# The gate of the first half step: sixteen float32 gate products on TensorE, replaced by row products that VectorE sums

## The chip, the cores and the metric

The kernel runs on one core of a Trainium2 chip. The metric is the device time of one execution in microseconds (us); a lower one is better. Times of several runs are given as their median with the lowest and the highest. One execution was taken by the hardware profiler; all rows below come from it.

## The reference

A two-layer backbone works on 512 latent tokens and 256 context tokens of width 1024, all in float32. Each layer is a half step of a gated feed-forward net, an attention (2-D neighbourhood attention in layer 0, windowed attention in layer 1), and a second half step. Each of these three is modulated by a shift, a scale and a gate, which come from one conditioning vector per stream (latent `c`, context `c_ctx`):

```
m = split(silu(c) @ w_mod[i] + b_mod[i], 9)            # nine vectors of 1024 per layer and stream
y = (silu(a) * v) @ w_out,  [a, v] = (h*(1 + m[1]) + m[0]) @ w_in
h = layer_norm(alpha*h + 0.5 * m[2] * y)               # m[2]: the gate of the first half step
```

The case is about `m[2]` of layer 0. It is a vector of 1024 for each of the two streams. It isn't needed to compute `y`, but it is needed to add `y` to `h`.

## The kernel before

All activations lie transposed in SBUF: 8 tiles of 128 features, 768 token columns each. The weights are streamed as units of 128 x 2048, each in four quarters of 256 KB; a quarter is loaded (L94), cast to a high part by ScalarE (L102) and a low part is taken off by GpSimd (L104). A product in float32 accuracy is three matmuls, high x high, high x low and low x high (L153 to L155). The high and low parts lie in rings of eight quarters each, so a new unit can be prepared only when an old one has been read to its end.

A half step (`ffn`) goes through the inner width in 11 chunks. A chunk has two units that give the `a` and `v` products (`av`, tiles `pa` and `pv`), of which the gated value `gh`/`gl` is made, and a third unit for the way down (`down`, tiles `pd`). Each of the eight output tiles of `down`, for each group of columns, is added to the stream `z` by VectorE with the gate as a factor (`accumulate`, L453). So the first instruction that needs the gate `m[2]` is the first accumulate of chunk 0. PSUM has eight banks, by tag: "mm" and "c" two each for `pa` and `pv`, "s" two, "t" and "o" one each. In this half step the outputs of `down` in chunk 0 go through "s", "s" and "t".

The modulation vectors are made in two ways. The first (`gemv`) multiplies on TensorE: a stationary 128 x 32 piece with both conditioning vectors, a moving 128 x 512 weight tile, eight products in four column strips; then ScalarE copies the bank out (L176), four small matmuls transpose it (L179), and VectorE adds the bias (L182). The shift and scale of the first half step are made like this before anything else can run. Its gate also is: `late_gate` calls `gemv_bg(0, 4)` and `gemv_bg(0, 5)`, for 512 columns each. These load eight tiles of 256 KB each into the six "t2" buffers (L189) and multiply at L172 into the bank "o".

The second way (`gemv_dve`) leaves TensorE alone. The weights lie transposed in memory, so a tile holds 128 outputs by 512 inputs. A conditioning row is loaded to all partitions into one of two "ln" buffers (L223), Silu puts it into a PSUM bank (L225; latent into "o", context into "t"), and VectorE multiplies tile and row and sums along the row in one instruction (L208):

```
x = nc.vector.tensor_tensor_reduce(out=junk[:], in0=w[:], in1=cb[st], scale=1.0, scalar=0.0,
                                   op0=ALU.mult, op1=ALU.add, accum_out=out[st])
```

`junk` is scratch, in the same two "ln" buffers. Each output tile takes one such product per stream and per half of the 1024 inputs. All products of one half run before the rows of the other half are loaded. The products are a queue `bg` that `tick()` works off, at a pace that spreads them over the chunks; outside the middle chunks (phase "T") their tiles use the "t2" buffers, inside it two buffers "wt" and `zspare`. Before, the remaining 48 vectors' tiles (24 to 71) of layer 0 are queued ahead of the first half step, 192 products in two batches, and the first are worked off in chunk 1.

The order of the work on each engine is written down before the run: the framework simulates the program, lets instructions that stand earlier in it go first among those that are ready in the simulation, and fixes each engine's order. SP issues nearly all loads, in such an order. After chunk 1, `bias_tables` loads a table for the attention through SP: 8 small loads (`xd`), then 16 broadcast copies in memory (`yd`, 252 KB each).

Of the kernel before, what the change touches and what calls it, by code (L numbers as in the profile page):

```python
# [38 lines left out]
def hybrid_kernel(ctx: ExitStack, tc: tile.TileContext, h0, cc, crow, wmod, wmodt, bmod, lnp, wst,  # L39
                  rpbp, nmask, sinks, ropec, rmat, ident, wmask, out):  # L40
    nc = tc.nc
# [8 lines left out]
    def bank(tag, nm):  # L50
        return pp.tile([P, 512], F32, tag=tag, name=nm, bufs=banks[tag])

    def t2(nm, tag="t2"):
        return tp.tile([P, 512], F32, tag=tag, name=nm, bufs={"t2": 6, "ln": 2, "sl": 2}[tag])
# [109 lines left out]
    def gemv(layer, ch, pieces, tag):  # L164

        nm = f"{layer}_{ch}"
        ps = bank(tag, f"gm{nm}")
        kt = 0
        for t in pieces:
            for j in range(t.shape[1]):  # L170
                q = kt % 4
                nc.tensor.matmul(ps[32 * q:32 * q + 32, :], c_sb[:, kt, :], t[:, j, :], start=kt < 4, stop=kt >= 4,  # L172
                                 tile_position=(0, 32 * q))
                kt += 1
        ev = t2(f"gev{nm}")
        nc.scalar.copy(ev[:], ps[:])  # L176
        pt = bank(tag, f"gt{nm}")
        for j in range(4):
            nc.tensor.matmul(pt[:, 2 * j:2 * j + 2], ev[:, j * P:(j + 1) * P], sel[:], start=True, stop=True)  # L179
        for a in range(2):  # L180
            t = ch * 2 + 8 * a if ch < 4 else ch * 4 + 2 * a
            nc.vector.tensor_tensor(out=mod[layer][:, t:t + 2, :], in0=pt[:, 4 * a:4 * a + 4].rearrange("p (t s) -> p t s", s=2),  # L182
                                    in1=bmod_sb[:, layer, t:t + 2, None].broadcast_to([P, 2, 2]), op=ALU.add)

    def gemv_bg(layer, ch):
        pieces = []
        for q in range(8):
            t = t2(f"wm{layer}_{ch}_{q}").rearrange("p (a b) -> p a b", a=1)
            nc.sync.dma_start(t[:], wmod[ch, q // 4, :, q % 4:q % 4 + 1, :])  # L189
            pieces.append(t)  # L190
        gemv(layer, ch, pieces, "o")

    bg, last, last_exp, wtq = [], [None], [None], [0]

    def gemv_dve(layer, *ranges):


        def products(t, half, cb, out):
            wtq[0] += 1
            nm = f"wt{layer}_{t}_{half}"  # L200
            if phase_of[0] != "T":
                w = t2(nm)
            else:
                w = zspare if wtq[0] % 3 == 0 else ph["T"].tile([P, 512], F32, tag="wt", name=nm, bufs=2)
            nc.sync.dma_start(w[:], wmodt[layer, t, half])
            for st in sorted(out):
                junk = t2(f"jk{layer}_{t}_{half}_{st}", "ln")
                x = nc.vector.tensor_tensor_reduce(out=junk[:], in0=w[:], in1=cb[st], scale=1.0, scalar=0.0,  # L208
                                                   op0=ALU.mult, op1=ALU.add, accum_out=out[st])
                behind(x, last[0])  # L210
                yield

        def steps():
            cb, now = {}, None
            for i, (t0, t1, streams) in enumerate(ranges):
                acc = tp.tile([P, 48, 2, 2], F32, tag="gacc", name=f"ga{layer}_{t0}", bufs=1)[:, 0:t1 - t0]
                for half in ((0, 1), (1, 0))[i % 2]:
                    if half != now:
                        now, cb = half, {}
                        for st in streams:  # L220
                            nm = f"cb{layer}_{t0}_{half}_{st}"
                            t = t2(nm, "ln")
                            nc.sync.dma_start(t[:], crow[st, half:half + 1, :].broadcast_to([P, 512]))  # L223
                            cb[st] = bank("ot"[st], nm)[:]
                            behind(nc.scalar.activation(cb[st], t[:], AF.Silu), last_exp[0])  # L225
                    for t in range(t0, t1):
                        yield from products(t, half, cb, {st: acc[:, t - t0, half, st:st + 1] for st in streams})
                n = len(streams)
                nc.vector.tensor_tensor(out=acc[:, :, 0, 0:n], in0=acc[:, :, 0, 0:n], in1=acc[:, :, 1, 0:n], op=ALU.add)
                nc.vector.tensor_tensor(out=mod[layer][:, t0:t1, 0:n], in0=acc[:, :, 0, 0:n],  # L230
                                        in1=bmod_sb[:, layer, t0:t1, None].broadcast_to([P, t1 - t0, n]), op=ALU.add)

        bg.append((sum(2 * len(st) * (t1 - t0) for t0, t1, st in ranges), steps()))

    pace = [0.0, 0.0]

    def tick():

        pace[1] += pace[0]
        while bg and pace[1] >= 1:  # L240
            pace[1] -= 1
            if next(bg[0][1], "end") == "end":
                bg.pop(0)
# [25 lines left out]
    def gate(layer, m, w):  # L269
        gt = cp.tile([P, DT, 2], F32, name=f"gt{layer}_{m}")  # L270
        nc.vector.tensor_scalar(out=gt[:], in0=mvec(layer, m), scalar1=w, scalar2=None, op0=ALU.mult)
        return gt
# [49 lines left out]
    def behind(x, y):  # L322

        if y is not None and x.ins.engine == y.ins.engine:
            tc.add_manual_dep(x.ins, y.ins.name, mybir.DependencyInfo(
                mybir.DependencyClass.NoSync, mybir.DependencyReason.DATA), reason="order")
# [489 lines left out]
    def constants():  # L816
        for t, src in ((lnp_sb, lnp), (nmask_sb, nmask), (rm_sb, rmat)):
            behind(nc.sync.dma_start(t[:], src[:]), loaded[0])
        nc.sync.dma_start(nsink[:], sinks[:].broadcast_to([P, NH]))
        nc.vector.tensor_scalar(out=nsink[:], in0=nsink[:], scalar1=-1.0, scalar2=None, op0=ALU.mult)  # L820
# [333 lines left out]
    with tc.tile_pool(name="pre", bufs=1) as fp:  # L1154
        open_av()
        for q in range(4):
            pieces = []
            for i in range(2):
                t = fp.tile([P, 4, 512], F32, tag="wm", name=f"wm0_{q}_{i}", bufs=7)
# [75 lines left out]
            write(norm)  # L1235

    def late_gate():
        for ch in (4, 5):
            gemv_bg(0, ch)
        constants()  # L1240

    def whole(x, head):

        return lambda gi: [f() for f in (x[:5] if gi == 0 else head)]
# [4 lines left out]
    l3 = [ln("l3", i, g, 1, 0, 1, 3, "o", True) for i, g in enumerate(g2)]  # L1249
    l4 = [ln("l4", i, g, 1, 1, 1, 6, ("mm", "o")[i]) for i, g in enumerate(g1)]  # L1250

    gemv_dve(0, (24, 40, (0, 1)), (40, 72, (0, 1)))
    ffn("0a", g2, lambda: gate(0, 2, 0.5), late_gate, whole(l0[0], l0[1][:1]), first,
        {(f, g): ps for f in range(2) for g, ps in zip(g2, opened[f])})
    plan(pq0_0_0=l0[1][1:2], pk0_1_0=l0[1][2:3], vn0_1=l0[1][3:5] + l0[0][5:] + l0[1][5:])
# [140 lines left out]
```

## Time and profile before

| | us |
|---|---|
| median of 3 runs | 2860.63 |
| lowest, highest | 2854.68, 2862.81 |
| the profiled execution, its own time | 2868.23 |
| its span | 2866.4 |

| engine | busy us | share of the span |
|---|---|---|
| TensorE, matmuls | 2728.1 | 95% |
| TensorE, weight loads | 2447.8 | 85% |
| VectorE | 1805.4 | 63% |
| ScalarE | 1213.4 | 42% |
| GpSimd | 1658.0 | 58% |

The span is the time from the first to the last instruction of the profiled execution; the execution's own time has a little around it. PE is TensorE with its matmuls, PEld its weight loads, which overlap them; DVE is VectorE, ACT ScalarE, POOL GpSimd, and SPq the queue in which SP issues transfers. PEclk is the granted clock of TensorE as a share of 2.4 GHz. In a row of the timeline, what stands in brackets is how long the engine was idle before, and what ended that. A float32 matmul of the gate is two instructions in the trace. Starts of matmuls are closer together than their durations, since they are pipelined.

### The profile page before, as it was taken

The page shows a single profiled execution, that of the slowest core. Times are in us where ns is not written, and L with a number is a line of the kernel's source. Part 1 is how long each engine was busy: PE and PEld are TensorE (multiplying, and loading weights), DVE is VectorE, ACT ScalarE, POOL GpSimd, SP SyncE. Part 2 cuts the span into 40 slices and gives each one's busy share as a digit, 9 for nine tenths or more (in the row PEclk, how much of TensorE's full clock was granted, in tenths as well). Part 3 has the DMA queues.
Part 4 walks back from the last instruction along what each step waited for, and adds up shares of the span by engine and source line. Part 5 has one row for each costly group of instructions (what it writes and reads, how often), then busy time and mean ns, then how long its engine had stood idle before and what let it go on. Part 6 is the DMA issues. An engine that isn't in the chain of part 4 may idle for free.

```text
span 2866.4 us, 48106 instructions
## 1 busy us (share of the span) xinstructions
PE 2728.1 (95%) x17122; PEld 2447.8 (85%) x17122; DVE 1805.4 (63%) x4124; ACT 1213.4 (42%) x2497; POOL 1658.0 (58%) x1488
## 2 busy tenths in 40 slices
PE   8999999999999989999999999999998998899997
PEld 5789899888888878999998899998886776888997
DVE  3286777585545676766654776666566667687744
ACT  4223333256454444434333534343246555444443
POOL 4357575375434455876744677765466444577763
PEclk9999999999999989999999999999999999899998
DMA  8525557432212212345462326466522111235562
GB/s 300 141 87 158 133 144 208 134 103 82 60 49 62 58 56 86 97 121 140 119 167 83 96 83 166 134 183 180 174 81 62 31 31 45 59 89 129 123 181 65
DMA packets 286016, 322.42 MB, mean 112 GB/s; under 512 B 28497, under 2 KB 174033, under 8 KB 284753
## 3 DMA queue, kind: packets, MB, share of 16 engines
q1 hardware_dynamic: 269936, 290.89, 34.2%
q0 software_dynamic: 15552, 28.32, 5.9%
q8 instruction: 135, 2.21, 0.3%
q14 instruction: 105, 0.85, 0.1%
q10 hardware_dynamic: 288, 0.14, 0.0%
HBM read 311.41 MB, written 12.25 MB: 113 GB/s over the span
## 4 chain that ended last, share of the span: by engine, by line
PE 52%; DVE 6%; DMA 2%; issue 2%; ACT 1%; POOL 1%; SPq 0%; DVEq 0%; POOLq 0%; ACTq 0%
PE pd1a L153 2%; PE pd0b L153 2%; PE pd1a L154 2%; PE pd0b L154 2%; PE pd0b L155 2%; PE pd1a L155 2%; PE wo L800 1%; PE pd1b L153 1%; PE pd1b L154 1%; PE pd1b L155 1%; DMA wr<-in_wst_dram 1%; PE tpw L791 1%; PE pa1a L153 1%; PE pa1a L154 1%; PE pv1a L153 1%
## 5 line engine op out<-in xcount | busy, mean ns | idle before, releaser
L104 POOL TENSOR_TENSOR wl<-wr,wh 128x512 fp32r<-128x512 f32 x308 | 404.0, 1328 | 298.4 <-ACT wh L102 238.4
L104 POOL TENSOR_TENSOR wl_s<-S,wh_s 128x512 fp32r<-128x512 f32 x202 | 268.4, 1366 | 60.5 <-ACT wh_s L102 59.7
L102 ACT CAST wh<-wr 128x512 fp32r<-128x512 f32 x308 | 186.7, 619 | 215.1 <-DMA wr<-in_wst_dram 62.2
L102 ACT CAST wh_s<-S 128x512 fp32r<-128x512 f32 x216 | 130.9, 620 | 322.4 <-POOL S L574 84.1
L208 DVE CUSTOM_DVE_ANT_0 jk<-wt,cb 128x512 f32<-128x512 f32 x303 | 200.4, 680 | 61.4 <-DMA wt<-in_wmodt_dram 52.1
L574 POOL TENSOR_TENSOR S<-wr,wr 128x512 f32<-128x512 f32 x108 | 146.9, 1360 | 148.6 <-DMA wr<-in_wst_dram 130.1
L104 POOL TENSOR_TENSOR wl_a<-wr,wh_a 128x512 fp32r<-128x512 f32 x120 | 159.1, 1376 | 24.9 <-ACT wh_a L102 24.5
L102 ACT CAST wh_a<-wr 128x512 fp32r<-128x512 f32 x162 | 100.4, 621 | 125.9 <-PE pd1b L154 18.3
L453 DVE SCALAR_TENSOR_TENSOR z<-pd0b,gt,z 128x256 f32<-128x256 f32 (+1 forms) x176 | 103.4, 602 | 62.2 <-PE pd0b L155 62.0
L453 DVE SCALAR_TENSOR_TENSOR z<-pd1a,gt,z 128x512 f32<-128x512 f32 (+1 forms) x168 | 99.8, 619 | 44.5 <-PE pd1a L155 43.3
L807 POOL TENSOR_SCALAR p<-p,l 128x512 f32<-128x512 f32 x64 | 44.6, 698 | 128.9 <-DVE l L906 120.5
L453 DVE SCALAR_TENSOR_TENSOR z<-pd0a,gt,z 128x512 f32<-128x512 f32 (+1 forms) x168 | 98.7, 618 | 29.5 <-PE pd0a L155 28.9
L319 POOL TENSOR_SCALAR z<-z,ag_None,ab_None 128x256 f32<-128x256 f32 (+1 forms) x78 | 63.5, 819 | 53.4 <-DVE uh L305 42.8
L208 DVE CUSTOM_DVE_ANT_0 jk<-zspare,cb 128x512 f32<-128x512 f32 x113 | 75.8, 679 | 15.6 <-DMA zspare<-in_wmodt_dram 15.6
L807 POOL TENSOR_SCALAR pw<-pw,l 128x512 f32<-128x512 f32 (+1 forms) x64 | 41.2, 645 | 74.4 <-DVE l L1097 33.0
L574 POOL TENSOR_TENSOR S<-S,wr 128x512 f32<-128x512 f32 x54 | 77.1, 1427 | 3.2 <-DVE x1b L557 0.7
L574 POOL TENSOR_TENSOR S<-wr,S 128x512 f32<-128x512 f32 x54 | 76.8, 1422 | 2.9
L905 ACT ACTIVATE p<-s,m 128x512 f32<-128x512 f32 x64 | 44.0, 688 | 77.3 <-DVE m L903 72.3
L453 DVE SCALAR_TENSOR_TENSOR z<-pd1b,gt,z 128x512 f32<-128x512 f32 (+1 forms) x98 | 56.8, 609 | 14.8 <-PE pd1b L155 12.3
L306 DVE TENSOR_TENSOR ul<-ufl,uh 128x256 fp32r<-128x256 f32 (+1 forms) x88 | 63.0, 722 | 2.3 <-ACT ufl L301 1.7
L301 ACT ACTIVATE ufl<-z,bi_None,sc_None 128x256 f32<-128x256 f32 (+1 forms) x86 | 54.7, 654 | 22.2 <-DVE z L438 21.9
L153 PE MATMUL pd0a<-gh0a,wh 128*128 128x512 f32 (+1 forms) x144 | 50.6, 365 | 8.3 <-DVE z L453 8.3
(1463 smaller groups left out, 10687.0 us busy)
## 6 DMA issues: line engine op xcount, KB each, us to landing
wr<-in_wst_dram SPq DMA_DIRECT2D x524, 256.0 KB
wt<-in_wmodt_dram SPq DMA_DIRECT2D x175, 256.0 KB
zspare<-in_wmodt_dram SPq DMA_DIRECT2D x65, 256.0 KB
wr_0b<-in_wst_dram SPq DMA_DIRECT2D x42, 256.0 KB
wr_1b<-in_wst_dram SPq DMA_DIRECT2D x42, 256.0 KB
wr_2b<-in_wst_dram SPq DMA_DIRECT2D x42, 256.0 KB
wr_3b<-in_wst_dram SPq DMA_DIRECT2D x42, 256.0 KB
wm<-in_wmod_dram SPq DMA_DIRECT2D x8, 1024.0 KB
```

The lines of the kernel that those rows point to most:

```text
L102: nc.scalar.copy(hi[:], src[:])
L104: eng.tensor_tensor(out=lo[:], in0=src[:], in1=hi[:].bitcast(F32), op=ALU.subtract)
L153: nc.tensor.matmul(ps, a[0], b[0], start=first, stop=False)
L154: nc.tensor.matmul(ps, a[0], b[1], start=False, stop=False)
L155: last_pe[0] = nc.tensor.matmul(ps, a[1], b[0], start=False, stop=last)
L208: x = nc.vector.tensor_tensor_reduce(out=junk[:], in0=w[:], in1=cb[st], scale=1.0, scalar=0.0, op0=ALU.mult, op1=ALU.add, accum_out=out[st])
L301: nc.scalar.activation(uf[:, :n], zs, AF.Identity, scale=s1, bias=s2)
L306: return hi, nc.vector.tensor_tensor(out=lo, in0=uv, in1=uo.bitcast(F32), op=ALU.subtract)
L319: nc.gpsimd.tensor_scalar(out=zs, in0=zs, scalar1=prm[2][:, d:d + 1], scalar2=prm[3][:, d:d + 1], op0=ALU.mult, op1=ALU.add)
L453: last[0] = nc.vector.scalar_tensor_tensor(out=zt(d, c0, c1), in0=pd, scalar=gt[:, d, st:st + 1], in1=zt(d, c0, c1), op0=ALU.mult, op1=ALU ...
L574: nc.gpsimd.tensor_tensor(out=t[:], in0=a[:], in1=b[:], op=o)
L807: nc.gpsimd.tensor_scalar(out=p, in0=p, scalar1=r, scalar2=0.0, op0=ALU.mult, op1=ALU.add)
```

## The change

The gate is no longer made by `gemv_bg`, which goes. `late_gate` puts the eight output tiles 16 to 23 (the gate's 1024 outputs) with both streams into the queue of VectorE's products, sets the pace to one product per tick and works the queue off on the spot: 32 products, with two rows loaded for each half. Only then come the constants and the queueing of the other 192 products, which stood ahead of the half step before. In the program all of this stands ahead of chunk 0.

```
-    def gemv_bg(layer, ch):
-        pieces = []
-        for q in range(8):
-            t = t2(f"wm{layer}_{ch}_{q}").rearrange("p (a b) -> p a b", a=1)
-            nc.sync.dma_start(t[:], wmod[ch, q // 4, :, q % 4:q % 4 + 1, :])
-            pieces.append(t)
-        gemv(layer, ch, pieces, "o")
...
     def late_gate():
-        for ch in (4, 5):
-            gemv_bg(0, ch)
+        gemv_dve(0, (16, 24, (0, 1)))
+        pace[0] = 1
+        while bg:
+            tick()
         constants()
+        gemv_dve(0, (24, 40, (0, 1)), (40, 72, (0, 1)))
...
-    gemv_dve(0, (24, 40, (0, 1)), (40, 72, (0, 1)))
     ffn("0a", g2, lambda: gate(0, 2, 0.5), late_gate, whole(l0[0], l0[1][:1]), first,
```

## Rows read from the trace of the kernel before

**Rows 1.** The page, its first part: busy time of each engine, share of the span.
```profile
PE 2728.1 (95%) x17122; PEld 2447.8 (85%) x17122; DVE 1805.4 (63%) x4124; ACT 1213.4 (42%) x2497; POOL 1658.0 (58%) x1488
```

**Rows 2.** Stretches of 20 us: length, busy us (instructions), PEclk, DMA share, GB/s.
```profile
core 0: us, PE busy (x) PEld busy (x) DVE busy (x) ACT busy (x) POOL busy (x), PEclk, DMA share, GB/s
60.00:80.00 20.00, 20.00 (x92) 12.21 (x90) 3.60 (x7) 6.25 (x13) 7.73 (x6) 1.00 0.42 120
80.00:100.00 20.00, 20.00 (x102) 13.76 (x101) 1.62 (x4) 2.16 (x4) 3.87 (x4) 1.00 0.32 97
100.00:120.00 20.00, 20.00 (x107) 16.60 (x106) 8.15 (x16) 6.08 (x11) 12.93 (x13) 1.00 0.50 80
...
140.00:160.00 20.00, 17.61 (x74) 14.35 (x75) 17.79 (x46) 3.37 (x6) 5.16 (x5) 0.73 0.62 200
```

**Rows 3.** Groups of TensorE's instructions from 60 to 110 us: busy us, mean ns.
```profile
L172 PE MATMUL gm<-wm,c_sb 128*32 128x512 f32 x32 | 12.4, 603 | 0.0
...
L179 PE MATMUL gt<-sel,gev 128*128 128x2 f32 x16 | 1.9, 240 | 0.0
```

**Rows 4.** TensorE in order of time, 63 to 110 us: start us, duration us, instruction.
```profile
63.28 0.28 PE L155 MATMUL pa0a<-uh,wl 128*128 128x256 f32 x1
63.41 0.28 PE L153 MATMUL pa0a<-uh,wh 128*128 128x256 f32 x1
63.61 1.05 PE L172 MATMUL gm<-wm,c_sb 128*32 128x512 f32 x2
64.59 0.38 PE L154 MATMUL pa0a<-ul,wh 128*128 128x256 f32 x1
...
74.70 0.39 PE L153 MATMUL pd0a<-gh0a,wh 128*128 128x512 f32 x1
74.93 0.40 PE L154 MATMUL pd0a<-gl0a,wh 128*128 128x512 f32 x1
...
92.39 0.39 PE L153 MATMUL pv0a<-uh,wh 128*128 128x512 f32 x1
92.70 1.91 PE L172 MATMUL gm<-wm,c_sb 128*32 128x512 f32 x12
94.55 0.50 PE L154 MATMUL pv0a<-ul,wh 128*128 128x512 f32 x1
...
103.20 0.40 PE L153 MATMUL pa0a<-uh,wh 128*128 128x512 f32 x1
...
109.07 0.40 PE L153 MATMUL pd0a<-gh0a,wh 128*128 128x512 f32 x1
```

**Rows 5.** TensorE in order of time, the first matmul after the stop.
```profile
141.89 0.80 PE L153 MATMUL pd0a<-gh0a,wh 128*128 128x512 f32 x1 [6.83 <-DVE z L453]
```

**Rows 6.** VectorE in order of time: the gate, two products, the product that waits.
```profile
105.61 0.24 DVE L271 TENSOR_SCALAR gt<-mod 128x16 f32<-128x16 f32 x1
...
125.97 0.69 DVE L208 CUSTOM_DVE_ANT_0 jk<-wt,cb 128x512 f32<-128x512 f32 x1 [0.67 <-ACT cb L225]
...
126.58 0.68 DVE L208 CUSTOM_DVE_ANT_0 jk<-wt,cb 128x512 f32<-128x512 f32 x1
...
140.13 0.69 DVE L208 CUSTOM_DVE_ANT_0 jk<-wt,cb 128x512 f32<-128x512 f32 x1 [9.65 <-DMA wt<-in_wmodt_dram]
```

**Rows 7.** SP's queue in order of time: start us, time to the end of the issues.
```profile
43.10 0.62 SPq L223 DMA_DIRECT2D cb<-in_crow_dram  x1
...
48.12 1.40 SPq L189 DMA_DIRECT2D wm<-in_wmod_dram  x2
...
71.18 5.99 SPq L94 DMA_DIRECT2D wr<-in_wst_dram  x4
...
116.46 12.21 SPq L826 DMA_DIRECT2D yd<-xd  x14
129.53 0.87 SPq L205 DMA_DIRECT2D wt<-in_wmodt_dram  x1
```

**Rows 8.** A stretch of 4 us, columns as in the 20 us stretches.
```profile
60.00:64.00 4.00, 4.00 (x24) 3.25 (x23) 2.42 (x5) 3.04 (x7) 2.59 (x2) 1.00 0.25 69
```

## The prediction

> **What bounds the kernel now.** I read the busy shares first: TensorE is busy for 95% of the span, VectorE for 63%, ScalarE for 42% [rows 1]. A share over the whole span does not say what a change in one stage is worth, so the second view is the table of 20 us stretches, for the stretch that the change touches. The reader is to see that TensorE is busy for all of the 60 us from 60 to 120 at a granted clock of 1.00, while VectorE works 3.60, 1.62 and 8.15 us of each 20 [rows 2]. Here TensorE is the bound and VectorE has 35 us to spare in the 40 us from 60 to 100 (40 - 3.60 - 1.62). The third view is TensorE's instructions in order of time. In this stretch one matmul starts as the one before lets it, 0.13 us apart at 256 columns (63.28 to 63.41) and 0.23 us at 512 (74.70 to 74.93), and nothing else comes between them but the gate's own products [rows 4]. So each of these that goes lets all that follows move forward.
>
> The first place where TensorE stops is at 134.7 us: the next matmul starts at 141.89, after 6.83 us of idle time that ends with an accumulate of VectorE (L453) [rows 5]. That accumulate stood in VectorE's queue behind a row product (L208) which began at 140.13, after 9.65 us of waiting for its weight tile [rows 6]. The clock fell to a mean of 0.73 in the stretch from 140 to 160 [rows 2].
>
> **The change part by part.** *Removed from TensorE:* 16 gate products, each in two passes, so 32 instructions of L172 in the stretch from 60 to 110, and two groups of eight small transposing matmuls at L179; they are busy for 12.4 and 1.9 us there [rows 3]. The busy time is the lower bound of what they take, 14.3 us; the gap that they make between their neighbours is the better measure. A single product: the matmul at 63.41 is followed by one at 64.59 instead of 0.13 us later, and that one lasts 0.38 us instead of 0.28, so 1.18 - 0.13 + 0.10 = 1.15 us [rows 4]. Ten of the 16 stand alone like this, by the twos in which L172 comes: 11.5 us. Six run together at 92.70 (x12): 92.39 to 94.55 is 2.16 us, less 0.23, and 0.11 for the longer neighbour: 2.0 us [rows 4]. The two transposing groups are taken at their busy time, 1.9 us [rows 3]. The sum is 11.5 + 2.0 + 1.9 = 15.4 us, all of it in time in which TensorE never waits.
>
> *Added to VectorE:* 16 weight tiles, each multiplied with two conditioning rows, 32 products. Two that follow each other start 0.61 us apart (125.97, 126.58) [rows 6], so 32 x 0.61 = 19.5 us. The cover is VectorE's 35 us of idle time [rows 2]; I cost them at nothing. With that cover gone, as where accumulates are due, each product delays one by 0.61 us.
>
> *Transfers:* 16 tiles of 256 KB go and 16 of the same size come, into the same six buffers. New are four broadcasts of the conditioning rows (two streams, two halves), each with a Silu into the banks "o" and "t". The rings are 25% busy from 60 to 64 us [rows 8], so I cost this at nothing; the wait that it could make is weighed next.
>
> *When the gate comes.* Before, it is there at 105.61 [rows 6]. After, the loads can be issued where the gate's loads stood, from 48.12 [rows 7]; the rings fall quiet at about 61 [rows 8], so the first half's 16 products run from about 61 to 71 (16 x 0.61). The second half's rows need the "ln" buffers that the products also use as scratch, so their loads are issued only then, on SP and behind the weight loads that hold it from 71.18 for 5.99 us: about 77 [rows 7]. No row shows how long such a load takes to land; it is bounded below by nearly nothing and above by 10.6 us, the time from the tile load issued at 129.53 to the product at 140.13 [rows 6, 7]. With 9.8 us for the second half the gate comes at 87 to 98; I take the early half, as the traffic of 60 to 64 is nearer to that at 77 than that of 130.
>
> *What TensorE does meanwhile.* Before, it ran from 63.41 to 109.07 without needing the gate; without 15.4 us of gate products it reaches the same point at 93.7 [rows 4]. Left then, before it must have the gate, is the rest of the second unit of the next chunk: 48 matmuls at 0.23 and 48 at 0.13 us, 17.3 us, of which some 5 lay between 103.20 and 109.07 [rows 4]. So its supply lasts to about 93.7 + 12 = 106, less 1.4 us for the one output tile (6 x 0.23) that can no longer use bank "t" so early: 104. The gate comes 6 to 17 us before that. The bound of this cost is nothing on one side and, on the other, what the slower rival below prices.
>
> *Moved:* the queueing of the 96 further products in two batches now stands behind the first 32. Their rows were loaded at 43.10 [rows 7], long before use; now they wait for the same scratch buffers, until the gate's products end, at 87 to 98. The second row needs bank "t", which the down products also use and which came free at about 125 (first product with it at 125.97 [rows 6]), so 110 in the new order; 12 us and more lie between, against a landing of at most 10.6. I cost it at nothing. SP's constants move behind the products and are used much later: nothing.
>
> *The stall at 134.7.* Its transfers (16 broadcast copies of the bias table, 14 of which hold SP from 116.46 for 12.21 us, with the next tile load at 129.53 behind them [rows 7]) follow weight loads that follow TensorE's progress, so I let the stall move with all the rest. Its price is 6.83 us of idle time [rows 5] and the clock: a mean of 0.73 over 20 us means 10.8 us at the lower level of 1.2 GHz (0.27 / 0.5 x 20), of which TensorE was idle for 2.4, so 8.4 us of work at half speed cost 4.2 us more [rows 2]. That is 11.0 us that the new order can give back, and I take none of it.
>
> *Sum.* The profiled execution took 2868.2 us with a span of 2866.4; less 15.4 gives 2852.8. The median of the three runs is 2860.6, 7.6 lower; less the same 15.4 it gives 2845.2. I predict 2845.
>
> **The rivals.**
>
> *Faster still.* Accumulates and products meet differently and the stall at 134.7 goes too. For it: the gate comes earlier than TensorE's own forward shift explains (up to 18 us against 15.4), so the first chunk's outputs leave bank "t" sooner and the next products can start ahead of the bias table's traffic. Against it: three tiles are all that can be loaded ahead, and the rest meets that traffic anyway. 2845 - 11 = 2834.
>
> *Most of it given back.* TensorE comes sooner to data that does not come sooner. For it: the tile load of 129.53 is paced by SP and by other transfers; if the product at 140.13 and the accumulate behind it do not move, or the second half of the gate lands late, TensorE idles for what it saved. Against it: the loads follow the release of weight buffers by TensorE itself. With half of 15.4 and the clock's 4.2 lost: 2845 + 8 + 4 = 2857, within 0.3% of before. The Trainium skill has a rule on this side (Perfetto Trace Analysis, "Identifying the Most-Contended Engine"): a high busy share of matmuls is a poor measure of closeness to the bound, and the share of weight loads is better. By that rule TensorE, whose weight loads are busy 12.21 of 20 us from 60 to 80 [rows 2], would have slack there and the removal would return nothing, 2860.6; the unbroken starts in [rows 4] speak against it, and it adds little to this rival's chance.
>
> *Slower.* The order on each engine is fixed before the run. If TensorE's order puts down products that need the gate ahead of the next chunk's products, it stands still until the real gate comes, however much other work there is. Place: the first accumulate after the gate. Price: the gate needs two loads in a row, the second half's rows and its last tiles; if both are as late as the wait of 9.65 us [rows 6], the idle time is 19.3 us, and the clock costs 4.2 more as at 140: 2845.2 + 23.5 = 2868.7, slower than before. It decides from 15.4 - 4.2 = 11.2 us of idle time on. For it: just this happened at 134.7, with one load. Against it: the rings are much quieter at 77. The Trainium skill says that VectorE's queue is strictly first in, first out (PSUM — Partial Sum Buffer, "Engine vs sequencer instructions"); the accumulate behind the product of 140.13 agrees, and the rule speaks for this rival.
>
> **How the numbers follow.** My forecast has a chance of 0.47, faster still 0.17, given back 0.22, slower 0.14. The forecast's own range is 2839 to 2851 (the stall a few us longer or shorter). The whole range reaches from 2831 (the full 11 us and 3 of spread) to 2866, which leaves out the worse part of the slower case. This kernel's measurement can tell 0.3%, 8.6 us, from no change: below 2852 is faster, 0.47 + 0.17 = 0.64; 2852 to 2869 the same, 0.22; slower 0.14.
>
> **What would show it.** Right: no L172 or L179 on TensorE after 50 us; TensorE busy without a gap from 60 to about 119; 32 products of L208 before the first accumulate, most between 60 and 98; the gate (L271) at 87 to 98; and the first matmul of each later stage 13 to 18 us earlier. Wrong: idle time of TensorE ahead of the first down products whose wait ends on VectorE; a product that waits for a row's Silu for more than 10 us; a stall near 119 longer than 6.83 us; or a shift of the later stages below 9 us.

## The result and the profile after

The changed kernel took 2844.02 us (median of 5 runs, 2841.37 to 2846.08) beside 2862.71 us for the kernel before: a ratio of 0.9939, 95% interval 0.9922 to 0.9956. A second series gave 2847.86 us (2846.78 to 2849.40) beside 2859.08, ratio 0.9962 [0.9949, 0.9975]. By these ratios the gain is 17 us in the first series and 11 us in the second; 2845 us was predicted, 15.4 us of gain.

The profiled execution took 2845.25 us with a span of 2843.3 us. In the changed kernel the lines past the removed function are 8 lower: the products are L200, the conditioning rows are loaded at L215 and put through Silu at L217, the gate is L263, the accumulate L445. The busy shares of the page, as in [rows 1]:

```profile
PE 2705.9 (95%) x17074; PEld 2440.1 (86%) x17074; DVE 1835.1 (65%) x4186; ACT 1215.3 (43%) x2499; POOL 1656.7 (58%) x1488
```

The shares hardly move: a gain of 0.5% in one stage can't be read from them. The table of 20 us stretches shows it, with the columns of [rows 2]:

```profile
60.00:80.00 20.00, 20.00 (x115) 17.55 (x114) 13.96 (x43) 6.20 (x12) 6.37 (x5) 1.00 0.69 221
80.00:100.00 20.00, 20.00 (x116) 17.57 (x116) 15.26 (x38) 7.05 (x14) 18.09 (x17) 1.00 0.54 100
100.00:120.00 20.00, 17.23 (x115) 15.64 (x113) 9.04 (x21) 4.31 (x9) 6.36 (x5) 1.00 0.57 188
120.00:140.00 20.00, 11.55 (x46) 9.43 (x47) 12.02 (x31) 1.91 (x4) 2.57 (x2) 0.74 0.71 228
140.00:160.00 20.00, 20.00 (x127) 18.11 (x126) 15.71 (x34) 4.97 (x10) 7.22 (x6) 1.00 0.32 93
```

From 60 to 100 TensorE is busy throughout, as before, but it starts 115 and 116 instructions there instead of 92 and 102, while VectorE works 13.96 and 15.26 us instead of 3.60 and 1.62 [rows 2]. The stop has moved from the stretch after 134.7 us into the two stretches from 100 to 140. VectorE in order of time (start us, duration us, instruction, idle time before it and what ended it):

```profile
58.60 0.68 DVE L200 CUSTOM_DVE_ANT_0 jk<-wt,cb 128x512 f32<-128x512 f32 x1
...
70.70 0.68 DVE L200 CUSTOM_DVE_ANT_0 jk<-wt,cb 128x512 f32<-128x512 f32 x1
...
77.06 0.69 DVE L200 CUSTOM_DVE_ANT_0 jk<-wt,cb 128x512 f32<-128x512 f32 x1 [5.67 <-ACT cb L217]
...
88.36 0.68 DVE L200 CUSTOM_DVE_ANT_0 jk<-wt,cb 128x512 f32<-128x512 f32 x1
...
90.36 0.95 DVE L263 TENSOR_SCALAR gt<-mod 128x16 f32<-128x16 f32 x1
91.43 1.41 DVE L445 SCALAR_TENSOR_TENSOR z<-pd0a,gt,z 128x512 f32<-128x512 f32 x2
...
127.98 0.69 DVE L200 CUSTOM_DVE_ANT_0 jk<-wt,cb 128x512 f32<-128x512 f32 x1 [11.89 <-DMA wt<-in_wmodt_dram]
```

The first half of the gate's products ends at about 71.3 us, the second waits 5.67 us for its rows, and the gate is there at 90.36 instead of 105.61 [rows 6]. Then comes the stop. TensorE in order of time, its last matmul ahead of the stop and its first ones behind it:

```profile
116.95 0.28 PE L155 MATMUL pd0a<-gh0a,wl 128*128 128x256 f32 x1
128.45 1.65 PE L153 MATMUL pd0a<-gh0a,wh 128*128 128x512 f32 x3 [11.22 <-ACT gh0a L472]
129.89 0.63 PE L154 MATMUL pd0a<-gl0a,wh 128*128 128x512 f32 x1
130.32 0.63 PE L155 MATMUL pd0a<-gh0a,wl 128*128 128x512 f32 x1
130.75 0.96 PE L153 MATMUL pd0a<-gh0a,wh 128*128 128x512 f32 x2
131.55 0.39 PE L154 MATMUL pd0a<-gl0a,wh 128*128 128x512 f32 x1
```

It idles 11.22 us where it was 6.83 [rows 5]. ScalarE's gh0a, named as the releaser, stood in ScalarE's queue behind a conversion that waited 12.99 us for weights:

```profile
127.29 0.62 ACT L102 CAST wh<-wr 128x512 fp32r<-128x512 f32 x1 [12.99 <-DMA wr<-in_wst_dram]
127.82 0.85 ACT L472 CAST gh0a<-pv0a 128x512 fp32r<-128x512 f32 x2
```

So two queues stand at once, VectorE's behind a weight tile (11.89 us, above) and ScalarE's behind a weight load. Both transfers were issued late, at 118.51 and 117.15, and were slow to be of use, 9.5 and 10.1 us after that. SP's queue, start and time to the end of the issues, as in [rows 7]:

```profile
70.81 0.94 SPq L215 DMA_DIRECT2D cb<-in_crow_dram  x2
...
100.90 15.48 SPq L818 DMA_DIRECT2D yd<-xd  x16
117.15 0.34 SPq L94 DMA_DIRECT2D wr<-in_wst_dram  x1
118.51 0.33 SPq L197 DMA_DIRECT2D wt<-in_wmodt_dram  x1
```

The bias table's copies start 15.56 us earlier than before (116.46), but now all 16 stand together and hold SP for 15.48 us instead of 12.21 for 14, and a weight load stands between them and the tile. So the tile load is issued only 11.02 us earlier (129.53 to 118.51), while TensorE comes to its stop 17.8 us earlier (from 135.06 to 117.23, each the first matmul's start less its idle time). Of each of these three differences 2.2 us are not the change's: by so much this run's matmuls were earlier at 50 to 60 us already.

To see what this does to the rest, each matmul of a kernel is set against the same matmul of the kernel before (the n-th of its line and tile), with both times counted from the kernel's first matmul. The median difference over a stretch is called the **lead** below, counted from its value at 50 to 60 us, just ahead of the change (the first 40 us differ between runs of one kernel, by the granted clock among other things: 0.86 in the first 20 us of before, 1.00 here). The lead of the changed kernel is 16.0 us from 100 to 120 us of before (15.6 from there to the stop of before), and 14.5 us from 160 to 250 us, behind the stop. In the second series it is 16.0 and 14.3 us. From 100 to 120 us it is 16.0 us in all five other traces that hold the change whole and nothing added on TensorE. How far the lead of one kernel differs between runs is seen below, where an edit left the order of the copies as it was: 14.8 us for the changed kernel and -0.5 us for the one before, from 160 to 250 us.

### The profile page after: what moved, and what is told of

The parts are those of the page before. It is cut to its first block, busy times and chain, and to the rows that moved or that the text cites. A ratio compares the mean times of both kernels' runs of the same rounds, so it can differ in the third digit from the quotient of the medians.

```text
span 2843.3 us, 48085 instructions
## 1 busy us (share of the span) xinstructions
PE 2705.9 (95%) x17074; PEld 2440.1 (86%) x17074; DVE 1835.1 (65%) x4186; ACT 1215.3 (43%) x2499; POOL 1656.7 (58%) x1488
## 4 chain that ended last, share of the span: by engine, by line
PE 53%; DVE 6%; DMA 2%; issue 2%; ACT 2%; POOL 1%; SPq 0%; DVEq 0%; ACTq 0%; POOLq 0%
PE pd0b L153 2%; PE pd1a L153 2%; PE pd0b L154 2%; PE pd0b L155 2%; PE pd1a L154 2%; PE pd1a L155 2%; PE wo L792 1%; PE pd1b L153 1%; PE pd1b L155 1%; PE pd1b L154 1%; PE tpw L783 1%; DMA wt<-in_wmodt_dram 1%; PE pa0b L153 1%; PE pa0b L154 1%; PE pa0b L155 1%
## 5 line engine op out<-in xcount | busy, mean ns | idle before, releaser
L200 DVE CUSTOM_DVE_ANT_0 jk<-wt,cb 128x512 f32<-128x512 f32 x334 | 220.3, 682 | 58.5 <-DMA wt<-in_wmodt_dram 52.2
L445 DVE SCALAR_TENSOR_TENSOR z<-pd0b,gt,z 128x256 f32<-128x256 f32 (+1 forms) x176 | 103.2, 603 | 60.1 <-PE pd0b L155 59.8
L445 DVE SCALAR_TENSOR_TENSOR z<-pd1a,gt,z 128x512 f32<-128x512 f32 (+1 forms) x168 | 100.0, 621 | 42.9 <-PE pd1a L155 41.7
L445 DVE SCALAR_TENSOR_TENSOR z<-pd0a,gt,z 128x512 f32<-128x512 f32 (+1 forms) x168 | 98.8, 623 | 28.3 <-PE pd0a L155 26.0
L200 DVE CUSTOM_DVE_ANT_0 jk<-zspare,cb 128x512 f32<-128x512 f32 x114 | 76.9, 680 | 27.8 <-DMA zspare<-in_wmodt_dram 18.2
L445 DVE SCALAR_TENSOR_TENSOR z<-pd1b,gt,z 128x512 f32<-128x512 f32 (+1 forms) x98 | 56.9, 610 | 14.0 <-PE pd1b L155 13.9
```

Of the source, the lines that this page charges most:

```text
L445: last[0] = nc.vector.scalar_tensor_tensor(out=zt(d, c0, c1), in0=pd, scalar=gt[:, d, st:st + 1], in1=zt(d, c0, c1), op0=ALU.mult, op1=ALU ...
```

## The experiments

All were timed in five rounds beside the kernel before.

**Half the outputs on TensorE, two ways.** The change is undone for outputs 16 to 19, with `gemv_bg` back in place; in the other kernel for 20 to 23 instead (`gemv_bg(0, 5)` and the range 16 to 20). The edit against the changed kernel:

```diff
-        gemv_dve(0, (16, 24, (0, 1)))
+        gemv_bg(0, 4)
+        gemv_dve(0, (20, 24, (0, 1)))
```

> The first half of the gate's outputs (16 to 19) stays on TensorE, the second (20 to 23) goes to VectorE. My theory: the gain is the removed TensorE time, 15.4 us for all, so half of it is left, 7.7 us: a ratio to the kernel before of about 0.9973 (the whole change measured 0.9939). Rival: the gain comes from the gate being there earlier (90.4 instead of 105.6 us); it would be there at least as early here, with 16 products fewer on VectorE, so the whole gain of 15 us or more is kept, about 0.994.

> The other half: outputs 16 to 19 go to VectorE, 20 to 23 stay on TensorE. In the trace of the kernel before the first half's eight products stand alone, the second half's partly together: by the gaps that they make, 8 x 1.15 + 0.95 = 10.2 us against 2.0 + 2 x 1.15 + 0.95 = 5.3 us. The first half kernel gained 6.1 us ahead of the stop (by its matmuls' starts against those of before) and gave some 4 back there. My theory: this one gains 9 to 11 us ahead of the stop and is 5 to 10 us faster than before in all, ratio 0.9965 to 0.998. But the second half's products may be ordered alone here: then 5 to 7 us ahead of the stop. Rival (half is half, wherever the products stand): the same as the first half kernel, ratio 0.9994.

Measured: 0.9994 [0.9981, 1.0008] for the first and 0.9983 [0.9967, 0.9999] for the second. The first expectation failed: half of the change brought nothing that can be told from no change. The second kernel's interval leaves out 1 by a hair, but so does one further down of a kernel whose edit moved nothing. Its main expectation, 9 to 11 us ahead of the stop, failed too; the other case that it named, products ordered alone, came. Ahead of the stop both have a lead of 5.7 us, little more than a third of 16.0. The eight products that stay on TensorE stand alone among full matmuls whichever half it is. TensorE in order of time, from the kernel with outputs 20 to 23 left on it (there are eight such pairs from 64.48 to 81.91 us, the last two among matmuls of 512 columns):

```profile
64.27 0.28 PE L153 MATMUL pa0a<-uh,wh 128*128 128x256 f32 x1
64.48 1.04 PE L172 MATMUL gm<-wm,c_sb 128*32 128x512 f32 x2
65.45 0.39 PE L154 MATMUL pa0a<-ul,wh 128*128 128x256 f32 x1
65.68 0.28 PE L155 MATMUL pa0a<-uh,wl 128*128 128x256 f32 x1
65.89 1.05 PE L172 MATMUL gm<-wm,c_sb 128*32 128x512 f32 x2
```

Each takes 1.15 us from its neighbours, so 8 x 1.15 and 0.95 for the transposing group, 10.2 us, stay, and 15.4 - 10.2 = 5.2 us go; measured 5.7. The other part of the miss is the stop: its idle time is 12.7 and 11.5 us here, and the lead behind it 2.1 and 3.8 us. The times, with intervals of 0.13 to 0.16% on either side, don't contradict those leads: 2.1 / 2860 is 0.07% (0.06% measured) and 3.8 / 2860 is 0.13% (0.17%).

**No gate products on either engine.** The gate is made of its bias alone (VectorE adds the bias to itself).

> Leaves the gate's products out altogether, on TensorE and on VectorE, with their loads; the gate is made of the bias alone, so it is there some 40 us earlier. My theory: the 32 products, their 16 tiles and the wait for the gate are covered by TensorE's other work, so the time is that of the changed kernel within 4 us (ratio 0.993 to 0.995). Rival 1 (an early gate is what gains): another 10 us or more, 0.990 or less. Rival 2 (the products' loads and VectorE time cost something that the removal had to pay for): 4 to 8 us faster than the changed kernel, 0.991 to 0.9925.

Measured: 2844.18 us, 0.9946 [0.9931, 0.996], the changed kernel's own time. The lead behind the stop (8.6 us of idle time here) is 16.3 us, 1.8 more than with the products. So VectorE's 32 products, with their loads, cost at most these 1.8 us and are nearly free, as the prediction had them.

**The changed kernel with 16 products of the removed shape put back on TensorE**, on data that is already on the chip, their result unused.

```diff
+        for i in range(2):
+            ps = bank("o", f"dm{i}")
+            for kt in range(8):
+                q = kt % 4
+                nc.tensor.matmul(ps[32 * q:32 * q + 32, :], c_sb[:, kt, :], z[kt][:, 0:512], start=kt < 4, stop=kt >= 4,
+                                 tile_position=(0, 32 * q))
+            ev = t2(f"dev{i}")
+            nc.scalar.copy(ev[:], ps[:])
         gemv_dve(0, (16, 24, (0, 1)))
```

> The changed kernel with 16 products of the same shape put back on TensorE, on tiles that are in SBUF already (their result is not used): only the TensorE time comes back, without loads. My theory: what a product takes depends on whether others stand beside it. Here all are ready at once, so they run in fours at 1.06 us each four, 4 to 5 us in all: about 2849, ratio 0.9955. Rival: a product takes 1.15 us of TensorE wherever it stands, 16 of them 15 to 18 us: the whole gain is gone, ratio 1.000.

Measured: 2849.61 us, 0.9964 [0.9952, 0.9976]. Not all 16 products ran where the removed ones did: nothing held them, and six ran from 39.75 to 46 us, ahead of the stretch from which the lead is counted. The lead ahead of the stop is 12.6 us, so the other ten cost 3.4 us, where the removed 16, with their transposing groups, cost 16.0. TensorE in order of time, the ten:

```profile
61.92 1.05 PE L1234 MATMUL dm<-z,c_sb 128*32 128x512 f32 x4
62.90 0.39 PE L153 MATMUL pa0a<-uh,wh 128*128 128x256 f32 x1
...
65.88 0.28 PE L153 MATMUL pv0a<-uh,wh 128*128 128x256 f32 x1
66.09 1.92 PE L1234 MATMUL dm<-z,c_sb 128*32 128x512 f32 x16
67.94 0.39 PE L154 MATMUL pv0a<-ul,wh 128*128 128x256 f32 x1
```

Sixteen instructions (eight products) that need no load stand together in 1.92 us, and two products in 1.05; one product alone, two instructions, takes 1.04. At 1.15 us for each product, as the rival had it, ten would have cost 11.5 us. What the change removes is dear because its products stand alone among large matmuls, and not because of their arithmetic. That they stand alone because their tiles land one by one is likely from how they are loaded, but no run here separates it from the order that was written down. The stop again takes its part: 13.1 us idle, lead 8.7 us behind it.

**The gate's 32 products made twice**, one after the other, in the changed kernel.

> The changed kernel with the 32 products of the gate made twice, one set after the other (only the second is used): nothing more on TensorE, 19.5 us more on VectorE, 16 tiles and 4 row loads more, and the gate later by 19.5 us and two reloads of rows of 5.7 us: about 121 instead of 90.4. My theory: TensorE's supply of work that needs no gate ends at about 104 to 106, so it stops for some 15 us there, with 4 more at the lower clock; the later stop at 117 (11.2 us and clock) is partly absorbed, since its transfers go on meanwhile: 2850 to 2862, ratio 0.996 to 1.000. Rival (VectorE's idle time covers any number of products, the gate's time does not matter): 2844, ratio 0.994. Rival (the stop at 117 is not absorbed): 2862 to 2866, ratio 1.000 to 1.002.

Measured: 2869.16 us, 1.0024 [1.0012, 1.0036]: slower than the kernel before, outside the first range and above the second. TensorE's first matmul behind its wait:

```profile
139.07 0.76 PE L153 MATMUL pd0a<-gh0a,wh 128*128 128x512 f32 x1 [31.71 <-DVE ga L200]
```

And the waits of VectorE's products that made the gate late (139.38 us, the last line, where 121 was expected):

```profile
79.40 0.69 DVE L200 CUSTOM_DVE_ANT_0 jk<-wt,cb 128x512 f32<-128x512 f32 x1 [5.31 <-ACT cb L217]
...
98.66 0.69 DVE L200 CUSTOM_DVE_ANT_0 jk<-wt,cb 128x512 f32<-128x512 f32 x1 [6.49 <-ACT cb L217]
...
123.28 0.69 DVE L200 CUSTOM_DVE_ANT_0 jk<-wt,cb 128x512 f32<-128x512 f32 x1 [13.45 <-ACT cb L217]
...
135.59 0.69 DVE L200 CUSTOM_DVE_ANT_0 jk<-wt,cb 128x512 f32<-128x512 f32 x1 [4.89 <-DMA wt<-in_wmodt_dram]
...
139.38 0.17 DVE L263 TENSOR_SCALAR gt<-mod 128x16 f32<-128x16 f32 x1
```

TensorE ran until 107.4 us (139.07 - 31.71) without the gate and then stood. It goes on 0.31 us ahead of the gate, and the profile names a product (L200) as what released it: it did not wait for the gate itself. By the kernel's order of banks this matmul opens the third output tile, in bank "t", where the conditioning row stands that the last product reads. The price is that of the slower rival within these 0.31 us, since the gate is made of the same products. The last two waits lie in the table's copies or just behind them, which a later gate runs into; the stop at 117 us is gone, absorbed in this one.

**The bias table later.** In the changed kernel the whole table (8 transfers that fill its source, 16 copies) is moved from chunk 1 to chunk 6.

```diff
-            if mid is not None and ci == 1:
-                bias_tables()
...
                 wpos[0] += 3
+                if mid is not None and ci == 6:
+                    bias_tables()
```

> The changed kernel with the bias table's loads and broadcast copies moved from behind chunk 1 to chunk 6. My theory: the stop of TensorE at 117 us (11.2 us idle, and some 3 at the lower clock) is the weight tile that waits behind the table's transfers; without them there it goes or shrinks to a few us, a gain of 8 to 14 us: about 2832 to 2836, ratio 0.990. Rival: chunk 1 asks for ten tiles with three buffers, and the stop stays whatever else is on the queue: 2844, ratio 0.994; or the table's copies make the same stop in chunk 6.

Measured: 2853.43 us, 0.9978 [0.9967, 0.999]. The stop at 117 us is gone and the lead from 160 to 250 us is 26.4 us, 11.9 more than the changed kernel's. But in chunk 6 the copies make a new stop. That stretch, with the columns of [rows 2]:

```profile
350.00:400.00 50.00, 38.74 (x199) 36.23 (x198) 19.92 (x53) 13.76 (x26) 21.26 (x19) 0.89 0.62 187
```

and GpSimd there, waiting for weights behind the copies:

```profile
372.19 1.26 POOL L566 TENSOR_TENSOR S<-wr,wr 128x512 f32<-128x512 f32 x1 [18.80 <-DMA wr<-in_wst_dram]
```

The lead falls to 9.1 us from 400 to 450. So the stop at 117 us comes from the table's transfers, and moving them whole is no gain.

**The copies spread over chunks 3 to 8.** The first form only wrote the copies at later places of the program, for the changed kernel and for the one before.

> The changed kernel; of the bias table only the 8 small loads stay behind chunk 1, its 16 broadcast copies are spread over chunks 3 to 8, three in a chunk (one in the last). With all of it in chunk 6 the stop at 117 went and gained 10.4 us there, and a new one in chunk 6 cost 18. My theory: three copies at a time are too few to hold a weight tile up for long, so the gain at 117 stays: 2844 - 8 to 10 = 2834 to 2836, ratio 0.990 to 0.9915. Rival: each copy costs about a sixteenth of what they cost together, 0.7 to 1.1 us wherever it stands: 2844 or more, ratio 0.994 to 0.997.

> The same spreading in the kernel before, with the gate on TensorE. My theory: the stop at 134.7 is the same mechanism and costs 11.0 us (6.83 idle and 4.2 of clock), so 8 to 11 us of gain, ratio 0.996 to 0.997. Rival (that stop comes from the gate being late at 105.6): no gain, 1.000.

Measured: 0.9939 [0.992, 0.9957] and 0.9984 [0.997, 0.9998], with the stops where they were (10.6 and 8.1 us idle). Both traces show the 16 copies issued together at the old place (from 100.45 and 114.77 us): nothing holds them in the order, and they are put ahead as soon as their source is filled. The second interval leaves out 1 all the same, so a difference of 0.2% in one series proves nothing. So nothing had been tested, and the edit was made again with each copy held behind the weight loads of its chunk:

```diff
-        for h in range(NH):
-            nc.sync.dma_start(yd[h], xd[h].rearrange("r c e -> r (c e)")[:, None, :].broadcast_to([8, 16, RW * 8]))
+
+    def bias_copies(heads):
+        for h in heads:
+            src = xd[h].rearrange("r c e -> r (c e)")[:, None, :].broadcast_to([8, 16, RW * 8])
+            behind(nc.sync.dma_start(yd[h], src), loaded[0])
...
                 wpos[0] += 3
+                if mid is not None:
+                    bias_copies(range(NH)[(ci - s0) * 3:(ci - s0) * 3 + 3])
```

> The changed kernel, with the 16 copies of the bias table held, three for each of the chunks 3 to 8, behind that chunk's weight loads; the eight transfers that fill the table's source stay where they are. Theory: the stop at 117 us is made by the 16 copies standing together ahead of the next row load and weight tile; three copies at a time stop nothing. Where all of the table was moved, the kernel was 10.4 us further ahead between 140 and 350 us, so 2844 - 10 = 2834 us, ratio to the kernel before 0.990, no idle time of TensorE above 5 us between 110 and 140. Rival A: the eight source transfers make the stop: idle 10 to 11 us near 117 still, 2844, ratio 0.994. Rival B: the copies cost TensorE the same wherever they stand (18 us for 16 in chunk 6, so 3.4 us for three): the stop goes, but 3 to 4 us are lost in each of five or six chunks, 2852, ratio 0.9965.

> The kernel before, with the same edit: the copies of the bias table held, three for each of the chunks 3 to 8. Theory: the stop at 134.7 us (6.83 us idle, 4.2 us of lost clock) goes and its price was 11.0 us: 2861 - 11 = 2850, ratio 0.996. Rival A (source transfers make the stop): still there, ratio 1.000. Rival B (copies cost the same wherever they stand): 2861 - 11 + 18 = 2868, ratio 1.0025.

Measured, the changed kernel with held copies: 2837.85 us, 0.9923 [0.9911, 0.9936]. The stop is gone, and no new one takes its place there:

```profile
100.00:120.00 20.00, 20.00 (x127) 17.91 (x125) 11.26 (x27) 6.27 (x12) 8.07 (x8) 1.00 0.34 84
120.00:140.00 20.00, 19.58 (x107) 16.59 (x107) 18.87 (x48) 3.50 (x7) 7.97 (x7) 1.00 0.63 205
```

The weight tiles now come in good time; in SP's queue a tile load issued at 117.39 us

```profile
117.39 0.33 SPq L197 DMA_DIRECT2D zspare<-in_wmodt_dram  x1
```

is used 3.6 us later, after a wait of 0.45 us on VectorE:

```profile
120.97 0.69 DVE L200 CUSTOM_DVE_ANT_0 jk<-zspare,cb 128x512 f32<-128x512 f32 x1 [0.45 <-DMA zspare<-in_wmodt_dram]
```

The kernel before with held copies: 2848.78 us, 0.9959 [0.9942, 0.9975], as the theory had it. Its stretches where the stop was:

```profile
120.00:140.00 20.00, 20.00 (x125) 17.69 (x125) 13.60 (x39) 7.19 (x13) 10.20 (x8) 1.00 0.55 163
140.00:160.00 20.00, 18.99 (x104) 15.97 (x104) 16.61 (x37) 4.05 (x7) 8.08 (x6) 1.00 0.42 127
```

Its lead from 160 to 250 us is 9.7 us, the price of the stop in the kernel before. With the stop gone from both, the change is worth 26.1 - 9.7 = 16.4 us in place (26.1 is the lead of the changed kernel with held copies). Since the eight transfers that fill the source stayed where they were, the stop comes from the 16 copies that stand together. Two things end with it that no run separates: that the copies hold SP's queue, and that loads behind them are slow to land. The held copies may not be quite free: between 350 and 600 us the lead falls by 2.9 us here, by 3.8 us in the kernel before with the same edit and by 2.8 us in the repetition below, but by 0.5 to 1.1 us in the three traces of the changed kernel with the copies at their old place. What takes these 2 to 3 us was not tried.

**The two versions side by side.**

> The changed kernel as it is, beside the version with the held copies on the same chip, to tell the two apart directly. 2844 us, ratio to the kernel before 0.994 by all theories, with the stop near 117 us of 10 to 12 us idle time.

> The version with the table's copies held in chunks 3 to 8, as before. Theory: the stop's removal is worth its whole price at 117 us, 10 to 12 us, also at the end: 2834 us, and 10 us less than the changed kernel beside it. Rival: later waits give half of it back, whatever stands at 117: 2839 us, 5 us less (the earlier runs lay 4.6 us apart by their ratios, 0.9923 and 0.9939, against different runs of the kernel before).

Measured: 2847.86 us, 0.9962 [0.9949, 0.9975], and 2840.67 us, 0.9937 [0.9916, 0.9957]: 7.2 us apart, between the two expectations, so that what the stop is worth at the end is not settled between 5 and 10 us. Behind its place it is worth 11.5 us again (lead 25.8 against 14.3). The version with held copies is the fastest, but its runs spread from 2832.96 to 2851.85 us, and what spreads them is not shown. Later stages are likely to have a part in it: in the profiled run 4.4 us of the lead go between 2400 and 2800 us.

## Why the prediction was right

- **TensorE as the bound, 15.4 us removed.** Right: 15.6 to 16.0 us of lead ahead of the stop in both series, 16.1 and 16.4 with the stops taken out on both sides. The share that each form has was right as well: products alone 1.15 us, together cheap (3.4 us for ten). That the first series came within 1 us of 2845 is luck all the same: the second, of the same kernel, lies 3.84 us from it. The Trainium skill (Perfetto Trace Analysis, "Identifying the Most-Contended Engine") says that the busy share of weight loads tells better than that of matmuls how close TensorE is to its peak. The trace agrees: with the small products gone, the weight loads' share from 60 to 80 rose from 12.21 to 17.55 of 20 us. But the prediction took the section to mean that TensorE had slack there, which it does not say; a low share can also mean that TensorE's time goes into small products, and here all of the removed time came back in place.
- **32 products on VectorE at nothing.** Right within 2 us: at 0.61 us apart they run in its idle time, and without them the lead grows by 1.8 us only, of which the stop's own length is a part.
- **The gate.** The steps came where they were put: first half done at 71.3 (71), the second half's first product at 77.06 (77 to 87.6), the gate at 90.36 (87 to 98, the early half). With the 2.2 us by which this run was ahead from the start they lie in the same ranges.
- **TensorE's supply.** Predicted to last until 104 us; the kernel with doubled products ran until 107.4, in a run that lay 2.7 us behind the changed kernel's (SP issues the second half's rows at 73.50, there at 70.81), so 104.7 on the changed kernel's times. The gate came 14 us before that, so its time decides nothing, and the slower rival had no place. Where the products ended later than the supply, TensorE stood as that rival had it and the kernel was slower, though the wait was for the bank that the last row holds, which the prediction had counted only as a supply shorter by 1.4 us. Such a stop is one of queues: the Trainium skill says that the queues of VectorE and ScalarE are strictly first in, first out (PSUM — Partial Sum Buffer, "Engine vs sequencer instructions"), and the trace agrees, with gh0a at 127.82 right behind the conversion that had waited 12.99 us.
- **The stop moves along unchanged.** The one term that was mis-sized. It moved (to 117 us; 119 predicted) but grew from 6.83 to 11.22 us of idle time, which the prediction had named as the wrong sign. Of its price of 11.0 us (6.83 + 4.2 of clock) 9.7 was measured in the kernel before; in the changed kernel it is 11.6, 11.9 and 11.5 by the three kernels without it (leads 26.1 and 26.4 against 14.5, 25.8 against 14.3). The idle time is 4.4 us longer, but the clock gives 2.7 us of that back: 0.74 in the stretch from 120 to 140 means 10.4 us at the lower level of 1.2 GHz, most of it while TensorE stood. The seven matmuls from 128.45 on take 3.10 us to the start of the one at 131.55, where at 0.23 us apart they would take 1.6, so 1.5 us were lost instead of 4.2. Both sums, 11.0 and 12.7 us, lie 0.8 to 1.3 us above what was measured; the kernels without the stop, which it is measured against, still idle 1.01 and 0.42 us in the same places. So the stop gave back 1 to 2 us of the gain (16.0 and 15.6 against 14.5 and 14.3 us of lead; 11.5 to 11.9 against 9.7 of price), where "transfers follow TensorE's progress" had promised none: counted from the same start, TensorE's stop moved by 15.6 us, the copies by 13.4 and the tile behind them by 8.8. So the mechanism of the rival "most of it given back" was at work, at about a sixth of its 12 us.
- **Later stages 13 to 18 us earlier.** 14.5 us by the lead behind the stop, and from 350 to 2800 us the lead stays between 12.8 and 18.1.

## What to carry to other kernels

A small product costs the engine far more alone among large matmuls (1.15 us) than in a group that is ready together (1.92 us for eight), so what its removal brings is read from the gaps around it, not from its busy time, and half of it need not bring half. A gain in one stage meets the next transfer that does not move as far: look at what stands in the DMA queue ahead of the next load and move that too, in small groups that are really held in the order. Compare the starts of matching instructions behind the change as well as the times at the end; here the first agreed within 0.5 us between three runs with the same order (14.3 to 14.8), while the times of one kernel lie up to 20 us apart (2844.55 to 2865.01 in one series). Look also at where the parts of an added piece of work really ran, before its price is divided by their number.

## What the runs showed of the hardware that was not expected

- A tile load of 256 KB was used 3.6 us after its issue where the copies were held, and 9.5 us after it (118.51 to 127.98) behind 16 copies from memory to memory. The share of busy DMA engines hardly tells the two apart: 0.81 from 117.39 to 120.97 in the first, 0.90 from 118.5 to 128 in the second. The broadcast rows, issued from 70.81, could be used at 77.06; among the copies, in the kernel with doubled products, rows issued from 114.55 were used at 123.28, at the end of a wait of 13.45 us.
- Sixteen copies of the table cost 11 to 12 us of TensorE's time in chunk 1, 17 us in chunk 6 (lead 26.4 to 9.1, from 160 to 250 and from 400 to 450 us), and made no such stop when they went three at a time; the 2 to 3 us that those kernels lose between 350 and 600 us are the most that can be put down to them.
- A stop's price in time is not its idle time: 6.83 us idle cost 9.7 us, 11.22 us idle 11.5 to 11.9. TensorE's clock fell to 1.2 GHz in both, and the shorter stop left more work to be done at that clock (4.2 us lost by the sum, against 1.5).
